# Storing a 4 KB result in two halves of 64 partitions, from two queues, in place of one store

## The chip, the cores and the metric

The kernel runs on one core of a Trainium2 chip. The metric is the device time of one execution in microseconds (us), given as the median of several executions on the same chip as the kernel it is compared with. A profile is one execution. Its span, from the first to the last instruction, is some 1.3 us shorter than the time of the execution. A store's *tail* means, throughout this document, the time from the end of VectorE's last accumulator read, when the result is complete, to the end of the span. The *issue* is the recorded instruction with which an engine starts a store, the *packets* are the pieces in which the DMA engines then move it, and the *landing* is the arrival of its last completion count at the semaphore. Where packets and landings are given to the nanosecond, they are read from the trace's own records. All runs of the comparisons were in the fast state and had a granted clock of 1.0; the one single run (`probe`) has no state, and none of its times is compared.

## The reference

```python
log_input: float32 [1024, 4096];  target: float32 [1024, 4096]
loss = np.exp(log_input) - target * log_input
return np.mean(loss, axis=-1).astype(np.float32)        # [1024]
```

Each partition holds 8 consecutive rows of the 1024, so the result is a tile of 128 partitions by 8 values, 4 KB, and each partition's 32 bytes lie next to those of the following partition in memory.

## The kernel before

SyncE loads both inputs in pieces that get smaller towards the end. ScalarE forms the exponentials and their row sums, and VectorE the products and theirs. ScalarE joins the sums of the first seven rows of each partition. VectorE's last instruction joins those of the eighth, so the store waits for it.

```python
out_v = out.rearrange("(p b) -> p b", b=nb)                     # 128 x 8
all_loss = nc.alloc_sbuf_tensor("all_loss", [P, nb], F32).ap()
# ... loads on SyncE; per row: exp on ScalarE, product on VectorE, join on ScalarE ...
            nc.vector.tensor_tensor_reduce(                     # the last piece of the last row
                out=place("t", lo, w + n_parts), ...,
                accum_out=all_loss[:, last_row : last_row + 1],
            ).wait_op(last_ready, 18, "sem-ge").then_inc(loss_done, 1)

    nc.sync.wait_ge(join_done, last_row)
    nc.sync.dma_start(out=out_v, in_=all_loss).wait_op(loss_done, 1, "sem-ge").then_inc(
        out_done, 16
    )
    used = landed + [last_ready, exp_done, prod_done, join_done, ones_done, loss_done]
    nc.sync.sem_clear(range(used[0].num, out_done.num))         # beside the flight of the store
    # ...
    nc.sync.wait_ge(out_done, 16).then_inc(out_done, -16)       # the end of the kernel
```

## Time and profile before

| | before |
|---|---|
| time, median of 6 runs beside the changed kernel | 84.02 us (83.98 to 84.13) |
| span of the profile | 82.5 us |
| end of VectorE's last accumulator read | 81.07 us |
| issue of the store, SyncE | at 81.10 us, 0.348 us long |
| first packet of the store | 0.843 us after the issue begins |
| tail | 82.545 - 81.071 = 1.474 us |

The kernel is bound by its loads, and the change can reach nothing of them. What it can reach is the tail. The issue is what SyncE itself spends, and the packets come well after it has ended. The lines of the profile that show this stand in the prediction below.

### The profile page before, as it was taken

How to read it: one execution, taken by the hardware profiler on the slowest of the kernel's cores; microseconds unless marked ns; L12 is line 12 of the kernel's file. 1: busy time of each engine (PE TensorE's matmuls, PEld its weight loads, DVE VectorE, ACT ScalarE, POOL GpSimd, SP SyncE). 2: the span in 40 equal slices, each digit the busy share in tenths (PEclk: the TensorE clock that was granted, in tenths of full speed). 3: DMA queues.
4: the chain of work that ended last, by engine and by line, in shares of the span. 5: the costliest groups of instructions: out<-in, count | busy, mean ns of one | idle time of the engine just before them, and what ended most of it. 6: DMA issues, size and time to landing. Idle time of an engine off the chain costs nothing.

```text
span 82.5 us, 131 instructions
## 1 busy us (share of the span) xinstructions
DVE 35.6 (43%) x22; ACT 33.2 (40%) x35; POOL 0.3 (0%) x5
## 2 busy tenths in 40 slices
DVE  0000000000000000000099999999369995993992
ACT  0500000000499920000000998979792496009460
POOL 0000000000000000000000000000000000000000
DMA  9289999929999992999599799799799999999960
GB/s 508 127 381 508 508 508 508 476 95 445 508 508 508 508 413 95 508 508 508 254 508 429 333 508 492 318 460 508 302 453 397 461 421 418 426 402 412 397 231 2
DMA packets 2016, 33.56 MB, mean 407 GB/s; under 512 B 352, under 2 KB 608, under 8 KB 1120
## 3 DMA queue, kind: packets, MB, share of 16 engines
q1 hardware_dynamic: 2016, 33.56, 95.8%
HBM read 33.55 MB, written 0.00 MB: 407 GB/s over the span
## 4 chain that ended last, share of the span: by engine, by line
DMA 72%; DVE 18%; issue 5%; SPq 3%; DVEq 0%
DMA t_big<-in_target_dram 49%; DMA x_big<-in_log_input_dram 23%; DVE t_big L175 17%; SPq L129 3%; DVE t_big L193 1%; DVE parts L175 0%; DVEq L192 0%; SPq L127 0%; DVE all_loss L193 0%
## 5 line engine op out<-in xcount | busy, mean ns | idle before, releaser
L175 DVE CUSTOM_DVE_ANT_0 t_big<-t_big,x_big 128x4096 f32<-128x4096 f32 (+3 forms) x8 | 26.2, 3308 | 43.5 <-DMA t_big<-in_target_dram 43.4
L155 ACT ACTIVATE e_dump<-x_big 128x4096 f32<-128x4096 f32 (+3 forms) x8 | 21.8, 2729 | 23.9 <-DMA x_big<-in_log_input_dram 23.6
L141 ACT ACTIVATE join_dump<-parts 128x2 f32<-128x2 f32 x7 | 1.4, 203 | 20.4 <-DVE parts L175 20.3
L175 DVE CUSTOM_DVE_ANT_0 t_mid<-t_mid,x_mid 128x4096 f32<-128x4096 f32 x2 | 8.8, 4424 | 2.0 <-DMA t_mid<-in_target_dram 2.0
L155 ACT ACTIVATE e_dump<-x_mid 128x4096 f32<-128x4096 f32 x2 | 7.1, 3568 | 0.0
L155 ACT ACT_TABLE_LOAD x1 | 1.3, 1283 | 2.9 <-PEq L48 2.9
L155 ACT ACTIVATION_READ_ACCUMULATOR e_dump<-x_big 128x1 f32 x8 | 1.5, 186 | 0.0
L141 ACT ACTIVATION_READ_ACCUMULATOR join_dump<-parts 128x1 f32 x7 | 1.3, 186 | 0.0
L175 DVE DVE_READ_ACCUMULATOR2_ANT parts<- 128x1 f32 x7 | 0.6, 84 | 0.0
L193 DVE CUSTOM_DVE_ANT_0 t_big<-t_big,x_big 128x390 f32<-128x390 f32 x1 | 0.6, 566 | 0.0
L155 ACT ACTIVATION_READ_ACCUMULATOR e_dump<-x_mid 128x1 f32 x2 | 0.4, 186 | 0.0
L175 DVE DVE_READ_ACCUMULATOR2_ANT t_big<- 128x1 f32 x3 | 0.2, 82 | 0.0
L136 POOL MEMSET x_big<- 128x6 f32 x1 | 0.1, 104 | 2.5 <-POOLq L48 2.5
L227 POOL MEMSET const-uint8-127<- 128x1 uint8 x1 | 0.1, 102 | 0.0
L227 POOL MEMSET const-bfloat16-1.0<- 128x1 bf16 x1 | 0.1, 101 | 0.0
L227 POOL MEMSET const-float32-0.0<- 128x1 f32 x1 | 0.1, 98 | 0.2 <-issue 0.2
L227 POOL MEMSET const-float32-1.0<- 128x1 f32 x1 | 0.1, 98 | 0.0
L193 DVE DVE_READ_ACCUMULATOR2_ANT all_loss<- 128x1 f32 x1 | 0.1, 82 | 0.0
## 6 DMA issues: line engine op xcount, KB each, us to landing
x_mid<-in_log_input_dram SPq DMA_DIRECT2D x1, 4096.0 KB, 49.9
t_mid<-in_target_dram SPq DMA_DIRECT2D x1, 4096.0 KB, 59.2
x_big<-in_log_input_dram SPq DMA_DIRECT2D x1, 2048.0 KB, 19.8
t_big<-in_target_dram SPq DMA_DIRECT2D x1, 2048.0 KB, 24.3
x_big<-in_log_input_dram SPq DMA_DIRECT2D x1, 1568.0 KB, 15.4
t_big<-in_target_dram SPq DMA_DIRECT2D x1, 800.0 KB, 17.0
t_big<-in_target_dram SPq DMA_DIRECT2D x1, 768.0 KB, 18.4
x_big<-in_log_input_dram SPq DMA_DIRECT2D x1, 384.0 KB, 18.9
```

Source lines behind the costliest of these rows:

```text
L129: dma = nc.sync.dma_start(out=place(what, lo, w), in_=src[:, lo : lo + w])
L136: nc.gpsimd.memset(big["x"][:, 4 * d : 4 * d + n_parts], -1.0).then_inc(ones_done, 1)
L141: nc.scalar.activation(out=join_dump[:, 2 * row : 2 * row + 2], in_=parts[:, 2 * row : 2 * row + 2], func=ACT_F.Copy, scale=inv_d, accum_o ...
L155: nc.scalar.activation(out=e_dump[:, col : col + w], in_=place("x", lo, w), func=ACT_F.Exp, bias=0.0, scale=1.0, accum_out=parts[:, 2 * ro ...
L175: nc.vector.tensor_tensor_reduce(out=place("t", lo, w), in0=place("t", lo, w), in1=place("x", lo, w), scale=-1.0, scalar=0.0, op0=ALU.mult ...
L193: nc.vector.tensor_tensor_reduce(out=place("t", lo, w + n_parts), in0=place("t", lo, w + n_parts), in1=place("x", lo, w + n_parts), scale= ...
L227: nc = _bacc.Bacc("TRN2", target_bir_lowering=False, num_devices=1)
```

## The change

The intent is to have two queues work on the store at once, each with half of the partitions. ScalarE has nothing left to do by then. A new semaphore tells SyncE that ScalarE's store is issued before SyncE clears the semaphores on which it waits.

```diff
+    issued = nc.alloc_semaphore("issued")
 ...
-    nc.sync.wait_ge(join_done, last_row)
-    nc.sync.dma_start(out=out_v, in_=all_loss).wait_op(loss_done, 1, "sem-ge").then_inc(
-        out_done, 16
-    )
-    used = landed + [last_ready, exp_done, prod_done, join_done, ones_done, loss_done]
+    for issuer, a, b in ((nc.scalar, 0, P // 2), (nc.sync, P // 2, P)):
+        issuer.wait_ge(join_done, last_row)
+        issuer.dma_start(out=out_v[a:b], in_=all_loss[a:b]).wait_op(
+            loss_done, 1, "sem-ge"
+        ).then_inc(out_done, 16)
+    nc.scalar.wait_ge(loss_done, 1).then_inc(issued, 1)
+    nc.sync.wait_ge(issued, 1)
+    used = landed + [last_ready, exp_done, prod_done, join_done, ones_done, loss_done, issued]
     nc.sync.sem_clear(range(used[0].num, out_done.num))
-    nc.sync.wait_ge(out_done, 16).then_inc(out_done, -16)
+    nc.sync.wait_ge(out_done, 32).then_inc(out_done, -32)
```

More of the change, by code (lines that the diff above doesn't have):

```diff
@@ L202 @@
             ).wait_op(last_ready, 18, "sem-ge").then_inc(loss_done, 1)
-    nc.sync.wait_ge(join_done, last_row)
-    nc.sync.dma_start(out=out_v, in_=all_loss).wait_op(loss_done, 1, "sem-ge").then_inc(
-        out_done, 16
-    )
-    used = landed + [last_ready, exp_done, prod_done, join_done, ones_done, loss_done]
+    for issuer, a, b in ((nc.scalar, 0, P // 2), (nc.sync, P // 2, P)):
[6 more added lines that the diff above has]
+    used = landed + [last_ready, exp_done, prod_done, join_done, ones_done, loss_done, issued]
+    assert all(used[0].num <= s.num < out_done.num for s in used)
     nc.sync.sem_clear(range(used[0].num, out_done.num))
-    assert all(used[0].num <= s.num < out_done.num for s in used)
-    nc.sync.wait_ge(out_done, 16).then_inc(out_done, -16)
+    nc.sync.wait_ge(out_done, 32).then_inc(out_done, -32)
 _INS = ['log_input', 'target']
```

## The prediction

> **What bounds the kernel now.** I read the page's first four parts before anything else, because the change touches only the last instruction that moves data, and the question is how much of the span that instruction owns. The header and the busy and slice rows, cut to those I use:
>
> ```profile
> span 82.5 us, 131 instructions
> ...
> DVE 35.6 (43%) x22; ACT 33.2 (40%) x35; POOL 0.3 (0%) x5
> ...
> DMA  9289999929999992999599799799799999999960
> GB/s 508 127 381 508 508 508 508 476 95 445 508 508 508 508 413 95 508 508 508 254 508 429 333 508 492 318 460 508 302 453 397 461 421 418 426 402 412 397 231 2
> ...
> DMA 72%; DVE 18%; issue 5%; SPq 3%; DVEq 0%
> ```
>
> No compute engine is busy half of the time, the DMA row is close to full until the last two of the 40 slices, and 72% of the chain that ended last is transfer. The kernel is bound by reading 33.55 MB; that ends before the store begins. So nothing that the change does can shorten the long part. The last slices are the tail, which I then read in the timeline from 79.6 us and in the store's own records:
>
> ```profile
> 80.38 0.08 DVE L175 DVE_READ_ACCUMULATOR2_ANT t_big<- 128x1 f32 x1
> 80.50 0.57 DVE L193 CUSTOM_DVE_ANT_0 t_big<-t_big,x_big 128x390 f32<-128x390 f32 x1
> 80.99 0.08 DVE L193 DVE_READ_ACCUMULATOR2_ANT all_loss<- 128x1 f32 x1
> 81.10 0.35 SPq L206 DMA_DIRECT2D out_dram<-all_loss  x1
> ```
>
> The columns are start, duration, engine and line. The last value of the result exists at 80.99 + 0.08 = 81.07 us, the store is issued 0.03 us later, and the issue takes 0.35 us (0.348 in the list of that line). From there to the end of the span nothing computes. The chain of waits stops at VectorE and doesn't show the store as a piece, so I followed it by cutting the last 1.45 us into four windows (engine columns are all idle; the last two columns are the share of the 16 DMA engines and GB/s):
>
> ```profile
> 81.10:81.45 0.35, 0.00 (x0) 0.00 (x0) 0.00 (x0) 1.00 0.00 0
> 81.45:81.94 0.49, 0.00 (x0) 0.00 (x0) 0.00 (x0) 1.00 0.00 0
> 81.94:82.14 0.20, 0.00 (x0) 0.00 (x0) 0.00 (x0) 1.00 0.39 21
> 82.14:82.55 0.41, 0.00 (x0) 0.00 (x0) 0.00 (x0) 1.00 0.00 0
> ```
>
> The store is thus 0.35 us of issue, 0.49 us in which no DMA engine has yet moved anything, 0.20 us in which all packets are moved, and 0.41 us until SyncE sees the completion count and the kernel ends. Only 0.20 us of these 1.45 us looks like something that depends on how much is stored. The transfer view of the last 1.5 us counts 144 packets: 128 of 32 bytes, one per partition, and one of 4 bytes on each of the 16 engines, which carries the completion.
>
> ```profile
> DMA packets 144, 0.00 MB, mean 3 GB/s; under 512 B 144, under 2 KB 144, under 8 KB 144
> ...
> out_dram<-all_loss SPq DMA_DIRECT2D x1, 4.0 KB, 1.4
> ```
>
> **What the Trainium skill says.** On "DMA: Bandwidth & Descriptors", section "Rules for kernel authors", there is a row on exactly this: of two transfers to disjoint partition halves it says "Don't bother", since both halves spread over the same 16 engines. Section "Issuing engines are not separate DMA queues" adds that issuing from several engines saves only sequencer time. The trace of before can't confirm the first, having one store, but agrees that there is hardly any sequencer time to save here: one issue, 0.35 us. The same page, "Why a DMA increments its semaphore by 16 and not by 1", gives the number of engines as the largest divisor up to 16 of the slowest dimension: 128 partitions give 16, which the 16 completion packets agree with, and 64 would still give 16, with 4 rows on each instead of 8. Last, "Perfetto Trace Analysis", section "DMA Instruction — HWDGE (DVE, Sync)", says that a block which makes the descriptors is shared and locked by one sequencer at a time, with the wait for it inside the recorded duration. The trace of before can only hint at such a cost: two issues directly behind one another on SyncE start 0.43 to 0.52 us apart and last 0.42 to 0.50 us, against 0.33 to 0.38 us for the first of a series. All of them are of one sequencer, so this is no proof of a lock between two.
>
> **The change part by part.**
>
> *Removed:* one issue of 128 rows. *Added:* two issues of 64 rows, on ScalarE and SyncE. Both wait for the same semaphore of VectorE's last instruction. ScalarE's last work ends at 80.24 + 0.19 = 80.43 us, so it has been idle for 0.6 us and can start when SyncE can; its wait for the seven joins is long past, since the last join ended at 77.21 + 0.19 = 77.40 us. Nothing of ScalarE's work is delayed.
>
> *What gets shorter, at best.* Each engine moves 4 rows instead of 8 of each half, but it gets both halves, so its total of data is the same. In the packet records one engine's eight 32-byte packets start about 6 ns apart, some 50 ns in all, and the engines begin one after another over the rest of the 0.20 us. If the two halves' descriptors are made at once, the latter could halve: my estimate is a saving of 0.20 / 2 = 0.10 us at most. If the issue time also depended on the rows it would shrink a little; but first issues of rows of 16,384 and of 3,136 elements and the store all take 0.33 to 0.38 us, so I count this as fixed and give nothing for it.
>
> *What gets longer.* There are now two completions, 32 increments from 160 packets (128 of data and 32 of completion) in place of 16 from 144. The later half sets the end. With 16 more packets of about 8 ns on 16 engines that is one more packet per engine, 0.01 us. If the second issuer waits for the first one's lock, its half begins up to one issue later: between 0.35 us (the duration of one issue) and 0.45 us (the spacing of issues in a series), less about 0.10 us because its own half is smaller, so +0.25 to +0.35 us. If ScalarE's issue is simply slower than SyncE's, being its first in the whole program, that adds directly; no trace here shows ScalarE issuing, and I allow 0.1 to 0.3 us.
>
> *The handshake.* ScalarE now signals that its issue is out, and SyncE clears the semaphores only then. In the kernel before the clear is at 81.50 us and lasts 62 ns, after which SyncE waits until 82.53 us. There is 82.53 - 81.56 = 0.97 us of slack. The handshake costs two semaphore instructions of 17 to 62 ns and some propagation, and at most a late ScalarE issue; it lies wholly beside the flight of the store. On the path: 0.
>
> *Sum.* No lock and an equal ScalarE: -0.10 + 0.01, about -0.1 us. A lock: +0.25 to +0.35 us. A slow ScalarE issue: +0.1 to +0.3 us, with or without the lock. I weigh a free overlap at 0.4, the lock at 0.4 and a slow ScalarE as the only thing at 0.2: 0.4 x (-0.1) + 0.4 x 0.3 + 0.2 x 0.3 = +0.14 us. On 84.07 us that is 84.2 us.
>
> **The rivals.**
>
> *The issue is hidden or halved, and the kernel gains.* This is presumably the intent. For it: the store is bare on the path, all 1.45 us. Against it: 0.35 + 0.49 + 0.41 = 1.25 us of these were quiet on the DMA engines, which suggests latency and not volume, and each half has to pay all of it in parallel with the other. It would make 83.9 to 84.0 us.
>
> *The halves serialize.* The sequence of issues on SyncE speaks for it a little, the Trainium skill for it plainly. Complete serialization of everything, with the second half going through the whole 1.45 us after the first, would make 85.5 us; nothing asks for that, since the second half isn't told to wait for the first. Serialized issue alone makes 84.3 to 84.4 us.
>
> *ScalarE is slow to issue, so that it becomes the end.* It could need to fetch or set something up for its first transfer. Against it: SyncE's first issue at time 0 took 0.38 us, hardly more than its later ones of 0.33. It makes 84.2 to 84.4 us, or up to 85 us if a setup of half a microsecond or more shows.
>
> *The start or the end of the launch changes.* A second queue is in use, and the time of a run is longer than the span (83.89 against 82.5 us in the profiled run, 1.4 us outside). If a queue costs something there it would not be seen in the span. I have no number for it and give it a few tenths in the upper end of the range.
>
> **Range and chances.** The runs of before lie within 84.0 to 84.13 us, so 0.1 us is noise to either side. The low end is the free overlap, 84.0, less that noise: 83.9. The high end is the lock together with a slow ScalarE, 84.07 + 0.35 + 0.3 = 84.7. Faster by over 2% means 1.68 us less, which is more than the whole store takes (1.45 us), so I give it 0.01. Slower by over 2% means 1.68 us more, more than a second store fully in series; only a large setup cost on ScalarE or on its queue could do this, 0.03. Within 2%: 0.96.
>
> **What would show each step right or wrong.** Right: the last accumulator read of VectorE at about 81.07 us as before; two issue records at 81.10 us, one on each engine, which overlap; first packets still about 0.84 us after the issue begins; the clear well before the last landing; and a span of 82.4 to 83.1 us. A lock shows as one of the two issues lasting 0.5 us or more, or its packets beginning some 0.3 us after the other's. A slow ScalarE shows as its issue lasting longer with SyncE's unchanged. If both halves' packets lie in a window of 0.1 us, the saving was real. I am wrong if the span moves by more than a microsecond, if the loads take another time than before, or if the time moves and the span doesn't.

## The result, and the profile after

The changed kernel takes 84.64 us (84.55 to 85.12, 6 runs) against 84.02 us (83.98 to 84.13, 6 runs). The ratio is 1.0078, with a 95% interval of 1.0056 to 1.0101. By the 2% rule this is "same", but it is a clear loss of about half a microsecond. A second series on another occasion gave 84.53 against 84.01 us.

The page of the profile after, in the lines that answer to those shown of before:

```profile
span 83.8 us, 134 instructions
...
DMA 72%; DVE 18%; issue 5%; SPq 3%; DVEq 0%
```

The shares are those of before. Next the timeline of the last stretch (start, duration, engine, line):

```profile
81.66 0.08 DVE L194 DVE_READ_ACCUMULATOR2_ANT all_loss<- 128x1 f32 x1
81.77 0.53 SPq L208 DMA_DIRECT2D out_dram<-all_loss  x1
81.77 0.54 ACTq L208 DMA_DIRECT2D out_dram<-all_loss  x1
```

Both issues start at once, as intended, but each now lasts over half a microsecond, against 0.348 us for the one store that moved all the rows. The same stretch cut into windows (the last two columns are the share of the 16 DMA engines and GB/s):

```profile
81.77:82.31 0.54, 0.00 (x0) 0.00 (x0) 0.00 (x0) 1.00 0.00 0
82.31:82.93 0.62, 0.00 (x0) 0.00 (x0) 0.00 (x0) 1.00 0.00 0
82.93:83.12 0.19, 0.00 (x0) 0.00 (x0) 0.00 (x0) 1.00 0.20 11
83.12:83.20 0.08, 0.00 (x0) 0.00 (x0) 0.00 (x0) 1.00 0.00 0
83.20:83.39 0.19, 0.00 (x0) 0.00 (x0) 0.00 (x0) 1.00 0.20 11
83.39:83.77 0.38, 0.00 (x0) 0.00 (x0) 0.00 (x0) 1.00 0.00 0
```

The two halves don't move together. One burst of packets lasts 0.19 us, then the engines are idle for 0.08 us, and then the other burst comes. By the packet records the first burst is SyncE's (first packet at 82.936 us) and the second ScalarE's (83.205 us, 0.269 us later). A burst is hardly shorter than the 0.20 us of the whole store before. The transfer view of the last 1.8 us shows the packets by queue, and the time from issue to landing:

```profile
q1 hardware_dynamic: 80, 0.00, 2.1%
q10 hardware_dynamic: 80, 0.00, 2.1%
...
out_dram<-all_loss SPq DMA_DIRECT2D x1, 2.0 KB, 1.7
out_dram<-all_loss ACTq DMA_DIRECT2D x1, 2.0 KB, 2.0
```

Each half has 64 data and 16 completion packets. SyncE's lands after 1.7 us and ScalarE's after 2.0 us, where the whole store took 1.4 us.

The tail grew from 1.474 us to 83.767 - 81.742 = 2.025 us, by 0.55 us. That is the loss in time, within its noise. This profile's span is longer by another 0.67 us because its last accumulator read ended at 81.74 instead of 81.07 us; this was the 85.12 us run, in which the loads came in late. The other runs of the same kernel have spans of 83.2 to 83.4 us. The moment at which the result is complete moves from profile to profile (81.07 to 81.35 us in the others of this study, `probe` left out), so below I compare tails, and times only as medians.

### The profile page after: what moved, and what is told of

The parts are those of the page before. It is cut to its first block, busy times and chain, and to the rows that moved or that the text cites. A ratio compares the mean times of both kernels' runs of the same rounds, so it can differ in the third digit from the quotient of the medians.

```text
span 83.8 us, 134 instructions
## 1 busy us (share of the span) xinstructions
DVE 35.6 (43%) x22; ACT 33.2 (40%) x35; POOL 0.3 (0%) x5
## 4 chain that ended last, share of the span: by engine, by line
DMA 72%; DVE 18%; issue 5%; SPq 3%; DVEq 0%
DMA t_big<-in_target_dram 49%; DMA x_big<-in_log_input_dram 23%; DVE t_big L176 17%; SPq L130 3%; DVE t_big L194 1%; DVE parts L176 0%; DVEq L193 0%; SPq L128 0%; DVE all_loss L194 0%
```

## The experiments

Twelve kernels ran. Each edit is against the changed kernel unless it says otherwise. Two theories stood at the start besides plain noise: **A**, two issues at the same moment hold one another up in something they share; **B**, ScalarE is slow to issue. A third, **C**, was that two stores cost more however they are issued.

### act_whole

```diff
-    for issuer, a, b in ((nc.scalar, 0, P // 2), (nc.sync, P // 2, P)):
+    for issuer, a, b in ((nc.scalar, 0, P),):
 ...
-    nc.sync.wait_ge(out_done, 32).then_inc(out_done, -32)
+    nc.sync.wait_ge(out_done, 16).then_inc(out_done, -16)
```

> The whole store, 128 rows, is issued by ScalarE alone, so no second issue is in flight. Theory A (two issues at the same moment hold one another up in something they share): ScalarE alone behaves as SyncE alone did; its issue lasts about 0.35 us instead of the 0.54 us it lasted beside SyncE's, first packets 0.84 us after the issue begins, tail from the last accumulator read of VectorE to the end 1.45 to 1.55 us, time 84.0 to 84.1 us. Theory B (ScalarE is slow to issue, or its queue is slow at first use): the issue still lasts about 0.54 us, packets begin some 1.4 us after it, tail about 2.0 us, time about 84.6 us. Theory C (two stores cost more however they are issued): as A here, 84.0 to 84.1 us.

Measured: 84.02 against 84.07 us, ratio 1.0004 (0.9978 to 1.0029); tail 1.506 us. The list of the store's line:

```profile
L208 ACTq DMA_DIRECT2D out_dram<-all_loss x1: 369/369/369, 81.1 to 81.1; - x1
```

ScalarE issues the whole store in 0.369 us (minimum, median and maximum are one issue), 0.02 us more than SyncE, and it is the first transfer that ScalarE issues in the program. Theory B falls. The handshake is still in this kernel, so it costs nothing either.

### sp_two_halves

```diff
-    for issuer, a, b in ((nc.scalar, 0, P // 2), (nc.sync, P // 2, P)):
+    for issuer, a, b in ((nc.sync, 0, P // 2), (nc.sync, P // 2, P)):
```

> Both halves are issued by SyncE, one after the other. Theory A: each issue is alone, the second begins 0.4 to 0.5 us after the first, as the spacing of the loads' issues was 0.43 to 0.52 us; tail 1.47 + 0.45 = 1.9 us, time 84.4 to 84.5 us, a little better than the changed kernel's 84.6. Theory B: the same as A, since no ScalarE issues. Theory C: at least as slow as the changed kernel, 84.6 us or more.

Measured: 85.0 against 84.07 us, ratio 1.0114 (1.0088 to 1.014), slower than A and B said (84.4 to 84.5 us); C had set only a floor of 84.6 us. The tail is 2.394 us.

```profile
L208 SPq DMA_DIRECT2D out_dram<-all_loss x2: 530/531/532, 81.2 to 81.8; - x2
```

Here no two issues coincide, and yet both last 0.53 us. That can't be one sequencer waiting for another.

### sp_one_half

```diff
-    for issuer, a, b in ((nc.scalar, 0, P // 2), (nc.sync, P // 2, P)):
+    for issuer, a, b in ((nc.sync, P // 2, P),):
 ...                                                # and out_done 16
```

> Wrong result on purpose: only rows 64 to 127 are stored, by SyncE; the other half of the output is never written. It measures what halving the rows saves. My prediction's term: the packet window shrinks from 0.20 to 0.10 us, time 83.9 us. What the changed kernel's trace suggests (each half's window was 0.17 us from first to last packet, against 0.19 us for the whole): the spread belongs to the 16 engines and not to the rows, saving of 0.02 us, time 84.0 us, issue still 0.35 us.

Measured: 84.31 against 84.07 us, ratio 1.0034 (1.0008 to 1.0059), with half of the output missing as intended. Storing half of the rows and nothing else is *slower* than storing them all; both of my accounts had it at 83.9 to 84.0 us.

```profile
L208 SPq DMA_DIRECT2D out_dram<-all_loss x1: 523/523/523, 81.3 to 81.3; - x1
82.43:82.62 0.19, 0.00 (x0) 0.00 (x0) 0.00 (x0) 1.00 0.21 11
```

The first line is the list of the issue, the second the window in which all the packets lie. The issue lasts 0.523 us with no other store anywhere. The first packet comes 1.167 us after the issue begins instead of 0.843 us, and the tail is 1.754 us, +0.28 us. Theory A's account of the long issues falls.

### stagger

```diff
-    for issuer, a, b in ((nc.scalar, 0, P // 2), (nc.sync, P // 2, P)):
+    for issuer, a, b in ((nc.sync, P // 2, P), (nc.scalar, 0, P // 2)):
+        if issuer is nc.scalar:
+            nc.sync.wait_ge(loss_done, 1).then_inc(go, 1)
+            nc.scalar.wait_ge(go, 1)
```

> SyncE issues its half, then signals, and only then does ScalarE issue the other half: two engines and two queues as in the changed kernel, but never two issues at the same moment. Theory A: both issues last 0.33 to 0.38 us, ScalarE's begins 0.4 to 0.45 us after SyncE's, its packets 0.84 us after that; tail 1.9 us, time 84.4 to 84.5 us, that is no slower than the changed kernel although the second issue begins 0.4 us later. Theory B: ScalarE's slow issue is added to the later start, tail 2.0 + 0.4 = 2.4 us, time about 85.0 us. Theory C: 84.6 us or more.

Measured: 84.93 against 84.07 us, ratio 1.0102 (1.0078 to 1.0125); tail 2.432 us. The timeline, and the two windows in which the packets lie (first SyncE's, then ScalarE's):

```profile
81.20 0.53 SPq L212 DMA_DIRECT2D out_dram<-all_loss  x1
81.86 0.52 ACTq L212 DMA_DIRECT2D out_dram<-all_loss  x1
82.37:82.55 0.18, 0.00 (x0) 0.00 (x0) 0.00 (x0) 1.00 0.22 12
83.04:83.22 0.18, 0.00 (x0) 0.00 (x0) 0.00 (x0) 1.00 0.22 12
```

Theory B's numbers, a tail of 2.4 us and 85.0 us, came out, but not its reason: SyncE's issue is as long as ScalarE's. Once more both issues are long although they don't overlap. One thing is different from the changed kernel, though. ScalarE's packets begin 1.180 us after its issue here, much as those of SyncE's lone half did (1.167 us), and 1.431 us after it in the changed kernel. So one store does wait for the other: of two 64-row stores issued at the same moment, the packets of the second come 0.25 us later than when it is issued 0.66 us after the first.

After these four I formed theory **D**: a 64-row store is by itself slow to issue, and two of them queue for their packets.

### column_halves

```diff
-    for issuer, a, b in ((nc.scalar, 0, P // 2), (nc.sync, P // 2, P)):
+    for issuer, a, b in ((nc.scalar, 0, nb // 2), (nc.sync, nb // 2, nb)):
 ...
-        issuer.dma_start(out=out_v[a:b], in_=all_loss[a:b])...
+        issuer.dma_start(out=out_v[:, a:b], in_=all_loss[:, a:b])...
```

> The same two issues at the same moment on the same two engines, each again 2 KB, but split by columns: each covers all 128 partitions with 4 of the 8 values (16 bytes). Theory D (formed after the first four runs: a store of 64 rows is by itself slower to issue than one of 128, 0.52 to 0.54 us against 0.35 to 0.37, and its packets start 1.17 us after the issue instead of 0.84; the second of two simultaneous stores then starts its packets another 0.27 us later): issues of about 0.35 us each, first packets at 0.84 us, the second half's at about 1.1 us, tail 1.47 + 0.27 = 1.75 us, time 84.3 us, half of the loss gone. Theory A (collision of the two issues is what stretches them): issues of about 0.54 us as in the changed kernel, tail 2.0 us, time 84.6 us.

Measured: 84.45 against 84.03 us, ratio 1.0047 (1.0034 to 1.006); tail 1.816 us.

```profile
L208 SPq DMA_DIRECT2D out_dram<-all_loss x1: 348/348/348, 81.2 to 81.2; - x1
L208 ACTq DMA_DIRECT2D out_dram<-all_loss x1: 380/380/380, 81.2 to 81.2; - x1
```

The same bytes from the same engines at the same moment issue in 0.348 and 0.380 us. So neither the moment nor the 2 KB makes the long issues. My explanation of the remaining loss missed: the packets of the two interleave, ScalarE's only 0.053 us behind. The last packet starts 1.09 us after the first issue begins, against 1.03 us before. The rest of the loss comes after the packets: from the start of the last packet to the last landing it takes 0.663 us, against 0.378 us before.

### act32_sp96 and act16_sp112

```diff
-    for issuer, a, b in ((nc.scalar, 0, P // 2), (nc.sync, P // 2, P)):
+    for issuer, a, b in ((nc.scalar, 0, 32), (nc.sync, 32, P)):      # act32_sp96
+    for issuer, a, b in ((nc.scalar, 0, 16), (nc.sync, 16, P)):      # act16_sp112
```

> The split by rows is uneven: 32 rows on ScalarE, 96 on SyncE. It asks how the issue time hangs on the number of rows. D1 (128 rows are a special fast case, any other number is slow): both issues last 0.52 to 0.54 us, time 84.6 us. D2 (the issue gets longer the fewer rows each engine has, in a line through 0.348 at 8 rows and 0.525 at 4): 0.44 us for 96 rows, 0.61 us for 32. Theory A: both about 0.54 us whatever the rows.

> 16 rows on ScalarE, 112 on SyncE. D1: both issues 0.52 to 0.54 us, time 84.6 us. D2 (the line of the run before): 0.39 us for 112 rows, 0.66 us for 16. If the second store's extra 0.27 us comes from making its packets one after the other, row by row, the smaller half should be quick to make, so that the packets of the one that comes second start sooner or end sooner; if it belongs to the 16 engines, it stays about 0.27 us.

Measured: 84.16 and 84.28 us against 84.03 us, ratios 1.0018 (1.0004 to 1.0032) and 1.0031 (1.0013 to 1.005); tails 1.627 and 1.635 us. The lines of the run with 32 and 96 rows; those of the other have the same durations:

```profile
L208 SPq DMA_DIRECT2D out_dram<-all_loss x1: 363/363/363, 81.2 to 81.2; - x1
L208 ACTq DMA_DIRECT2D out_dram<-all_loss x1: 396/396/396, 81.2 to 81.2; - x1
```

Both forms of my theory of the rows fall. It isn't that anything other than 128 is slow (D1), nor that fewer rows are slower (D2): 16, 32, 96 and 112 rows all issue in 0.36 to 0.40 us. Nor does the second store's packets' delay depend on its rows; it is 0.04 and 0.05 us here and not 0.27 us, and the packets of the two interleave.

### act_early_columns

```diff
             join(row - 1, k + 1)
+            nc.scalar.dma_start(out=out_v[:, 0 : nb - 2], in_=all_loss[:, 0 : nb - 2]).wait_op(
+                join_done, last_row, "sem-ge"
+            ).then_inc(early_done, 16)
 ...
+    nc.sync.wait_ge(early_done, 16)
+    nc.sync.dma_start(out=out_v[:, nb - 2 : nb], in_=all_loss[:, nb - 2 : nb])...   # in place of both halves
```

> Two stores on the two queues, but not at the same moment and both of 128 rows: ScalarE stores the first 6 columns when the seventh join is done, some 3.6 us before the end, and SyncE the last two at the end. Theory D: SyncE's issue lasts 0.35 us, its tail is 1.45 to 1.47 us as before the change, time 84.0 to 84.1 us: a second store and a second queue cost nothing of themselves. If two stores cost more however they are issued (C), 84.3 us or more. It could be slower for another reason: 8-byte packets, or the early store delaying a load by some hundredths.

Measured: 84.01 against 84.03 us, ratio 1.0002 (0.9989 to 1.0014); tail 1.475 us, SyncE's issue 0.348 us. A second store on ScalarE's queue costs nothing when it is out of the way (it was issued at 77.64 us and took 3.2 us to land beside the loads). Theory C falls. As a version this is no better than the kernel before: a final store of two columns has the same tail as one of eight.

### after_again

No edit.

> The changed kernel once more, unedited: is its profile typical? In the first profile the loads ended 0.67 us later than in the profile of before, in a run of 85.12 us where the others took 84.55 to 84.75. Expected: 84.6 us; both issues of 0.52 to 0.55 us, ScalarE's packets only after SyncE's, tail from the last accumulator read to the end 2.0 us, against 1.47 us before.

Measured: 84.53 against 84.01 us, ratio 1.0063 (1.0043 to 1.0083); tail 2.030 us. The issues last 0.525 and 0.543 us as in the first profile, to the nanosecond, and ScalarE's packets again begin 0.269 us after SyncE's, 1.431 us after its own issue. The tail repeats; only the late loads of the first profile didn't.

### act48_sp80

```diff
-    for issuer, a, b in ((nc.scalar, 0, P // 2), (nc.sync, P // 2, P)):
+    for issuer, a, b in ((nc.scalar, 0, 48), (nc.sync, 48, P)):
```

> Nearly even halves, 48 rows on ScalarE and 80 on SyncE, so that neither has 64. Theory E (64 rows are a slow case of their own; 128, 112, 96, 32 and 16 rows all issued in 0.35 to 0.40 us): issues of 0.36 and 0.40 us, packets of both in one window from 0.86 to 1.06 us after the issue, tail about 1.7 us, time 84.15 to 84.3 us, as with 32 and 96 rows. Theory G (what is slow is any split near the middle, since then the two generations of packets are equally long and get in one another's way): issues of about 0.53 us, 84.6 us.

Measured: 84.15 against 84.01 us, ratio 1.0017 (0.9999 to 1.0034); tail 1.616 us. The list of issues and the windows:

```profile
L208 SPq DMA_DIRECT2D out_dram<-all_loss x1: 363/363/363, 81.1 to 81.1; - x1
L208 ACTq DMA_DIRECT2D out_dram<-all_loss x1: 396/396/396, 81.1 to 81.1; - x1
```

```profile
82.00:82.22 0.22, 0.00 (x0) 0.00 (x0) 0.00 (x0) 1.00 0.37 19
82.22:82.73 0.51, 0.00 (x0) 0.00 (x0) 0.00 (x0) 1.00 0.00 0
```

A nearly even split is not slow to issue (G falls), and the packets of both halves share one window of 0.22 us. Moving 16 rows from one half to the other takes away 0.41 us of the changed kernel's 0.55 us. What is left comes with two stores ending together: the quiet stretch after the packets is 0.51 us here and was 0.41 us before. By the records, the last landing comes 0.491 us after the last packet starts, against 0.378 us before (+0.11 us), and the last packet itself comes 0.03 us later; together 0.14 us. Why the landing is later is not shown. In all these runs both stores count on one semaphore, so a wait of their writes can't be told from a wait of their counts; no run gave each store a semaphore of its own.

### probe

This one is an edit of the kernel before. ScalarE issues seven small stores of a zeroed tile one after the other, and the real store overwrites them. I judged that they would fit into 20 us; beside the loads the first four took 8 to 24 us each to land, so that the exponentials started at 64 us and the run took 101.08 us. The time says nothing, but the durations of the issues are what was wanted.

```diff
+    probes = [(0, 128, 8), (0, 64, 8), (0, 48, 8), (32, 96, 8), (0, 80, 8), (0, 64, 4), (0, 128, 8)]
+    for m, (a, b, c) in enumerate(probes):
+        if m:
+            nc.scalar.wait_ge(probed, 16 * m)
+        nc.scalar.dma_start(out=out_v[a:b, 0:c], in_=scratch[a:b, 0:c]).then_inc(probed, 16)
 ...
+    nc.sync.wait_ge(probed, 16 * len(probes))        # ahead of the real store
```

> The kernel before, with seven small stores issued by ScalarE one after the other in the first 20 us, in which it waits for its first load; each waits until the one before has landed, and the real store overwrites them all. In order: 128 rows, rows 0 to 63, rows 0 to 47, rows 32 to 95, rows 0 to 79, rows 0 to 63 with 4 of the 8 values, 128 rows. Theory E: issues of 0.37, 0.54, 0.40, 0.54, 0.40, 0.54, 0.37 us: it is the number 64, and neither the first row nor the bytes. If it is the alignment to a half of the partitions, rows 32 to 95 take 0.40 us. If it is the bytes (2 KB), the 64 rows of 4 values take 0.40 us. The loads run beside, so all may be a little longer; the two of 128 rows are the control.

The timeline, in the order of the list above:

```profile
3.11 0.39 ACTq L158 DMA_DIRECT2D out_dram<-scratch  x1
26.65 0.54 ACTq L158 DMA_DIRECT2D out_dram<-scratch  x1
41.32 0.34 ACTq L158 DMA_DIRECT2D out_dram<-scratch  x1
49.63 0.56 ACTq L158 DMA_DIRECT2D out_dram<-scratch  x1
60.51 0.33 ACTq L158 DMA_DIRECT2D out_dram<-scratch  x1
61.90 0.50 ACTq L158 DMA_DIRECT2D out_dram<-scratch  x1
63.60 0.36 ACTq L158 DMA_DIRECT2D out_dram<-scratch  x1
```

The second, fourth and sixth line are those of 64 rows, and they alone take half a microsecond or more: rows 0 to 63, rows 32 to 95, and rows 0 to 63 with half of the bytes. 48, 80 and 128 rows take 0.33 to 0.39 us. It goes with the number 64, in one program on one engine, and with neither the first row nor the bytes.

### sp_48_rows

```diff
-    for issuer, a, b in ((nc.scalar, 0, P // 2), (nc.sync, P // 2, P)):
+    for issuer, a, b in ((nc.sync, 80, P),):
 ...                                                # and out_done 16
```

> Wrong result on purpose: only rows 80 to 127 are stored, by SyncE, so that what fewer rows save is measured without the slow case of 64. My prediction's term said that the 0.20 us of packets shrink in proportion: 48 of 128 rows save 0.12 us, 83.9 us. If the spread belongs to the 16 engines: the packet window stays 0.16 to 0.18 us, the issue 0.36 us, tail 1.45 us, time 84.0 us.

Measured: 84.03 against 84.01 us, ratio 1.0 (0.9985 to 1.0015); tail 1.427 us, with the other rows of the output missing as intended. From the first to the last packet's start it is 0.163 us, against 0.191 us for all 128 rows. Leaving out 80 of 128 rows thus shortens the tail by 0.05 us, 0.03 us of it in the packets, and nothing that the time can show.

## Why the prediction was right or wrong

The measured 84.64 us lies inside the range of 83.9 to 84.7 us, near its top, and "within 2%" held. The size was 0.62 us in the first series and 0.52 us in the second, against a predicted +0.14 us worked out and a point of 84.2 us.

**That nothing outside the tail moves** was right. The changed kernel's loss is its tail: +0.55 us in both of its profiles. A launch cost of the second queue isn't there (act_whole and act_early_columns both use it, at 84.02 and 84.01 us).

**The handshake at 0** was right. In the profile after, the clear comes at 82.40 us, ahead of the first landing at 83.29 us, and act_whole has it for free.

**"My estimate is a saving of 0.20 / 2 = 0.10 us at most"** was an upper limit, but it entered the sum as an expected gain, and that was wrong. The burst's length hardly depends on the rows: from the first to the last packet's start it is 0.191 us for 128 rows, 0.170 us for a lone 64 and 0.163 us for 48. The share of rows may be taken from a window only if something shows that the window scales with them.

**"So I count this as fixed and give nothing for it"**, said of the issue time, is the step that failed. The argument used issues that differed only in the length of a row; all had 128 rows. With 64 rows the issue takes 0.52 to 0.54 us, the first packet comes 0.32 us later, and the tail of a lone half is 0.28 us longer. This is half of the loss, and sp_one_half shows it with no other store in flight. No number in the trace of before could have told it, as it has no store or load of 64 rows, and neither theory D1 nor D2 would have guessed it from its neighbours.

**The lock, "+0.25 to +0.35 us"**, had the right size, in part by luck. The second half's packets come 0.269 us after the first's, and 0.25 us later than they do when ScalarE issues 0.66 us after SyncE. The second sign that I gave, packets some 0.3 us behind the other's, came true. The first, one of the two issues lasting 0.5 us or more, pointed to the wrong thing: both issues last that long, and they do so without the other beside them (0.523 us in sp_one_half, 0.524 us for ScalarE in stagger). What waits isn't the recorded issue but the packets after it. And it is so long only for two stores of 64 rows issued at the same moment; for pairs of other sizes the delay is 0.04 to 0.05 us. The size was worked out from the spacing of issues on SyncE, which isn't what happened. It was also misread a little: the second issue of a series starts 0.37 to 0.38 us after the first, twice, so the spacings run from 0.37 and not from 0.43 us. And 0.10 us was taken off for the smaller half, of which only 0.02 us was there. That one store's packets wait for the other's is shown by its effect; what they wait for isn't.

**The slow ScalarE, "0.1 to 0.3 us"**, was wrong. It is 0.369 against 0.348 us, 0.02 us.

**The cost of more completions, "0.01 us"**, was too small where the two stores end together: +0.11 us in act48_sp80. In the changed kernel it doesn't show, because the halves come one after the other: 0.356 us from its last packet to its last landing, against 0.378 us before.

The sum as measured: 0.28 us for a store of 64 rows, and 0.27 us for the second half behind the first, are 0.55 us, and the tail grew by 0.55 us. That the time lies in the range is therefore luck. The range's top was the lock with a slow ScalarE, 0.35 + 0.3 us. The 0.3 us for ScalarE wasn't there, and it covered the 0.28 us of the 64 rows, which the prediction had left out. The point of 84.2 us, with 0.10 us of gain counted in, was about 0.4 us too low.

What stays open is *why* 64 rows are slow. The trace records the stores of 64 and of 96 rows in the same form, with only the count of rows different (`dst_num_elem=[64,1]` and `[96,1]`, `dst_elem_size=32` in both). Rows that were tried: 16, 32, 48, 80, 96, 112 and 128 are quick, 64 is slow; both engines, three first rows (0, 32, 64) and two row lengths (16 and 32 bytes) agree. Nothing was tried for loads.

## What to carry to other kernels

Of this small store's 1.45 us from issue to end, 1.25 us passed with no packet moving, and none of the five ways of issuing the result as two stores at the same moment came out ahead of one store (84.15 to 84.64 us, against 84.01 to 84.03): look for how the window of the packets scales before counting on half. If a store must be split, compare the issue record of the new shape with the old one by itself, since a shape can be slow for no visible reason (here 64 partitions: +0.28 us on the tail), and avoid that shape or move the early part well ahead of the end. A long issue record beside another engine's isn't yet a sign of the two waiting for each other; one run with the other taken away tells it.

## What the Trainium skill lacked or had wrong

- "DMA: Bandwidth & Descriptors", "Rules for kernel authors", advises against two transfers to partition halves because they serialize. The advice holds (84.64 against 84.02 us). Its reason is only half of it here: 0.27 us come from one half behind the other, 0.28 us from the 64 rows themselves, and with 48 and 80 rows the packets share one window and the loss is 0.14 us in the tail.
- No page that I found says that a store of 64 partitions is slower to issue than one of 48 or 80: 0.52 to 0.54 us against 0.36 to 0.40 us in the final stores, with the first packet at 1.17 us instead of 0.84 us. The number of engines that "Why a DMA increments its semaphore by 16 and not by 1" gives (16 for both) fits the 16 completion packets of each store, and doesn't tell the two apart.
- "Perfetto Trace Analysis", "DMA Instruction — HWDGE (DVE, Sync)", places the wait for a shared, locked block inside the recorded issue. In these runs two issues at the same moment are hardly longer than alone (0.348 and 0.380 us together, 0.348 and 0.369 us alone, for 128 rows); the one long wait for each other that the runs show before the packets lies after the record: ScalarE's first packet comes 0.25 us later with 64 rows.
- No page that I found gives a cost for two stores that complete together: the last landing came 0.491 us after the last packet started, instead of 0.378 us, with 48 and 80 rows, and 0.663 us with two stores of 16-byte pieces of the same rows.
